# A convolution and attention trunk: tanh for sigmoid in the gate, norm sums on TensorE, first-half gate products on VectorE

## The chip, the cores and the metric

One core of one Trainium2 chip. The metric is the device time of one execution of the whole program in microseconds; the engines are called by the names of the profile: PE (TensorE), DVE (VectorE), ACT (ScalarE), POOL (GpSimd) and SP (SyncE, which issues most DMAs).

## What is computed

Two pre-norm residual layers over 1024 tokens with 16 meta tokens ahead (T = 1040 columns), model width 1024: a Conformer convolution layer, then a differential attention layer, then a last norm. The change lies in the convolution layer alone (CONV_WIDTH 2048, 31 taps):

```python
def conv_mixer(h, w_in, dw_kernel, dw_bias, ln_gain, ln_bias, w_out):
    proj = jnp.einsum("bld,dc->blc", h, w_in)
    u, g, z = jnp.split(proj, 3, axis=-1)
    v = u * jax.nn.sigmoid(g)
    v = lax.conv_general_dilated(v, dw_kernel[:, None, :], window_strides=(1,),
        padding=[(CONV_KERNEL - 1, 0)], dimension_numbers=("NWC", "WIO", "NWC"),
        feature_group_count=CONV_WIDTH) + dw_bias
    v = jax.nn.silu(layer_norm(v, ln_gain, ln_bias))
    return jnp.einsum("ble,ed->bld", v * jax.nn.silu(z), w_out)

# in the trunk, for layer i:
hn = rms_norm(h, norm_gain[i])
h = h + conv_mixer(hn, ...)
```

## The kernel before

Channels lie on partitions, tokens along the free axis. Every matmul operand is split into a high part (`hh`, `wh`, `b` hi: a rounded copy made by ACT) and a low part (`hl`, `wl`, `b` lo: the difference, made by `lo_part` on DVE or POOL), and `passes` issues three matmuls for each product. The tile scheduler sets the order of every engine's instructions from the written order and from priorities: `SP_R`, `HP` and `WP` are offsets that move what stands under them ahead. Each engine runs its list strictly in order.

*Start.* The 8 tiles of x (`x0` to `x7`) come in three chunks of tokens (348, 346, 346 columns). `unscaled` splits a chunk of raw x, `statistics` squares it and adds the squares over channels for the first RMS norm (`SUE` says for each chunk and tile whether an add runs on POOL, G, on DVE, V, or as a matmul with ones, P), `first_strips` (p) projects tile 0's g and u from the raw chunk, and `scaled` writes x times norm and gain and splits that again, for all later projections. `ORDER` gives the sequence of these steps. `rstd_from` turns the sums into a reciprocal root: a table estimate on ACT and a Newton step on DVE.

*Convolution loop.* For each of 16 tiles of 128 channels PE projects g and u; ACT takes the sigmoid `sig` of g; DVE multiplies it by u into `vr`, the gated input, kept as even and odd tokens. The 31 taps are split by parity: DVE runs the even ones and part of the combined ones (`ev`, `co`), ACT multiplies an odd tap into `pr` and POOL adds it to `pb`. PE also projects z; `z_gate` takes silu(z) on ACT and writes it to memory (`sz_d`), to be loaded later as `szr`. POOL adds the outputs up over tiles in `hsum` (the last tile's add is DVE's).

*Transition.* The tokens are treated in two halves. `channel_sums` makes means and variances on PE, `center` subtracts the mean on DVE and squares on ACT, `token_scale` makes the reciprocal root. `y_part(k, 0, ...)` multiplies by it (DVE), takes silu (ACT) and multiplies by `szr` (DVE for the numbers in `YM`, else POOL); `szr` tiles hold two channel tiles each and there are two of them. `operand` splits the result into b hi (ACT) and b lo (DVE). The first half's sixteen `y_part` are written first, then sixteen `operand`; then the output projection's eight strips `c0` to `c7` follow, each with two weights of eight channel tiles (`wh48`/`wl48` and so on). While the first half is multiplied, the second half is centred and made ready.

The table functions of ACT lie in sets that a table load of the engine exchanges; the program before has 36 such loads.

## Time and profile before

| | us |
|---|---|
| median of three runs | 1486.27 (1485.87 to 1486.83) |
| the profiled execution | 1487.72 |
| its span | 1485.9 |
| PE busy in the span | 1420.5 (96%) |
| DVE busy | 1139.7 (77%) |
| ACT busy | 898.3 (60%) |
| POOL busy | 861.4 (58%) |

The convolution layer takes the first 810 us or so, attention the next 530, the output projection the rest. The shares are averages over stages with different limits: in the convolution loop POOL and DVE are nearly full, in attention they are not. A line of a timeline gives start and length in us of a run of like instructions; the bracket at its end is the idle time of that engine ahead of it and what ended it.

### The profile page before, as it was taken

Reading aid. Unit: us, or ns where it says so; the run is one execution under the profiler, and the core shown is the slowest. Engines: PE = TensorE matmul, PEld = TensorE weight load, DVE = VectorE, ACT = ScalarE, POOL = GpSimd, SP = SyncE. Lnnn points to the kernel's source line nnn. Section 1 sums busy time; section 2 is a strip of 40 time slices with the busy share of each in tenths; the row PEclk is TensorE's granted clock in tenths of the full one; section 3 lists DMA queues with packets and bytes.
Section 4 is the critical chain, followed back from the end, with each engine's and each line's share of the span. In section 5 each row is a group of like instructions: output and inputs, shape, how many; then the busy total and the mean of one; then the engine's idle time right before and its main releaser. Section 6 shows DMA issues by size and latency. Waiting matters only on the chain.

```text
span 1485.9 us, 24104 instructions
## 1 busy us (share of the span) xinstructions
PE 1420.5 (96%) x8788; PEld 1330.1 (90%) x8788; DVE 1139.7 (77%) x2102; ACT 898.3 (60%) x1618; POOL 861.4 (58%) x677
## 2 busy tenths in 40 slices
PE   8899999999999999699999999999999999998997
PEld 6799899999999999699999877988889899897887
DVE  8999999989999989768645411477788787876774
ACT  5576666656565657746423511568778787787651
POOL 6499999999999942425113600525254354353572
PEclk9899999999999999799999999999999999999999
DMA  5011102111121232545444543322322322338642
GB/s 180 29 67 48 56 30 86 44 43 57 43 64 51 94 107 72 177 139 185 150 152 150 170 136 100 95 72 77 100 70 83 112 79 75 86 102 259 204 135 78
DMA packets 79928, 150.82 MB, mean 101 GB/s; under 512 B 6977, under 2 KB 46402, under 8 KB 78786
## 3 DMA queue, kind: packets, MB, share of 16 engines
q1 hardware_dynamic: 64802, 123.01, 26.0%
q0 software_dynamic: 5728, 17.04, 3.6%
q10 hardware_dynamic: 9280, 9.23, 1.9%
q8 instruction: 69, 1.13, 0.3%
q14 instruction: 49, 0.40, 0.1%
HBM read 106.73 MB, written 34.01 MB: 95 GB/s over the span
## 4 chain that ended last, share of the span: by engine, by line
PE 50%; POOL 19%; DVE 12%; issue 8%; ACT 7%; DMA 4%; ACTq 0%; POOLq 0%; DVEq 0%; SPq 0%
POOL pb L502 17%; PE c L209 8%; PE v L209 6%; PE z L209 6%; PE k L209 5%; PE q L209 4%; PE ao L209 4%; PE za L209 4%; PE o L209 3%; PE s L974 2%; PE tp L1008 2%; PE s L975 2%; DVE wl L159 1%; DMA a<-ya_d 1%; PE u L209 1%
## 5 line engine op out<-in xcount | busy, mean ns | idle before, releaser
L502 POOL TENSOR_TENSOR pb<-pr,pb 128x521 f32<-128x521 f32 (+1 forms) x272 | 388.2, 1437 | 15.7 <-ACT pr L501 1.1
L501 ACT ACTIVATE pr<-vr,chn 128x521 f32<-128x521 f32 x224 | 150.7, 724 | 115.6 <-POOL pb L502 115.0
L209 PE MATMUL c<-b,wh 128*128 128x260 f32 x1024 | 191.0, 289 | 11.0 <-DVE b L159 10.7
L191 ACT ACTIVATE wh<-wf 128x1024 fp32r<-128x1024 f32 x115 | 121.1, 1053 | 113.1 <-PE c L209 63.7
L515 DVE SCALAR_TENSOR_TENSOR ev<-vr,chn,ev 128x520 f32<-128x520 f32 x240 | 180.8, 754 | 1.3
L209 PEld LDWEIGHTS c<-b,wh 128*128 128x128 f32 x1024 | 162.9, 194 | 11.9 <-DVE b L159 11.2
L209 PE MATMUL g<-hp,wh 128*128 128x346 f32 (+1 forms) x752 | 149.2, 328 | 12.3 <-DVE sig L469 4.5
L159 DVE TENSOR_TENSOR wl<-wf,wh 128x1024 fp32r<-128x1024 f32 x81 | 130.7, 1613 | 36.4 <-ACT wh L191 35.2
L209 PE MATMUL u<-hp,wh 128*128 128x346 f32 (+1 forms) x752 | 149.7, 321 | 3.6 <-ACT sz L433 2.2
L209 PE MATMUL c<-b,wl 128*128 128x260 f32 x512 | 147.5, 290 | 5.5 <-DVE wl L159 5.5
L209 PEld LDWEIGHTS g<-hp,wh 128*128 128x128 f32 x752 | 125.8, 192 | 16.8 <-ACT n_r L234 4.7
L209 PE MATMUL z<-hp,wh 128*128 128x346 f32 (+1 forms) x768 | 135.7, 321 | 2.0 <-ACT sig L466 1.9
L159 POOL TENSOR_TENSOR wl<-wf,wh 128x1024 fp32r<-128x1024 f32 x34 | 84.1, 2473 | 92.0 <-ACT wh L191 43.7
L515 DVE SCALAR_TENSOR_TENSOR od<-xs,wc,od 128x520 f32<-128x520 f32 x176 | 132.3, 752 | 0.0
L209 PEld LDWEIGHTS u<-hp,wh 128*128 128x128 f32 x752 | 124.5, 188 | 4.9 <-ACT sz L433 2.4
L209 PEld LDWEIGHTS z<-hp,wh 128*128 128x128 f32 x768 | 124.2, 188 | 2.7 <-ACT sig L466 2.2
L982 ACT ACTIVATE p<-p,st 128x272 f32<-128x272 f32 (+7 forms) x128 | 100.5, 785 | 36.3 <-DVE st L977 35.6
L209 PEld LDWEIGHTS c<-b,wl 128*128 128x128 f32 x512 | 99.7, 195 | 6.3 <-DVE wl L159 6.2
L685 POOL TENSOR_TENSOR total<-hsq,total 128x520 f32<-128x520 f32 x12 | 20.7, 1724 | 117.8 <-ACT hsq L684 117.8
L209 PE MATMUL v<-wv,g 128*128 128x512 f32 x352 | 83.5, 394 | 0.0
L209 PE MATMUL g<-hp,wl 128*128 128x346 f32 (+1 forms) x376 | 81.9, 323 | 0.0
L974 PE MATMUL s<-k,q 128*128 128x256 f32 (+6 forms) x224 | 76.7, 347 | 3.7 <-DVE st L977 3.7
(295 smaller groups left out, 3525.7 us busy)
## 6 DMA issues: line engine op xcount, KB each, us to landing
wf<-conv_in SPq DMA_DIRECT2D x48, 512.0 KB, 3.5
wf<-conv_out SPq DMA_DIRECT2D x32, 512.0 KB, 3.8
wf<-attn_in SPq DMA_DIRECT2D x32, 512.0 KB, 3.6
wf<-attn_out SPq DMA_DIRECT2D x17, 512.0 KB, 3.6
sz_d<-sz ACTq DMA_DIRECT2D x32, 260.0 KB, 3.8
szr<-sz_d SPq DMA_DIRECT2D x16, 520.0 KB, 4.6
v<-v_d POOLq DMA_DIRECT2D x8, 1024.0 KB, 5.4
ya_d<-yb SPq DMA_DIRECT2D x28, 256.0 KB, 2.5
```

The costliest lines, as they stand in the source:

```text
L159: return eng.tensor_tensor(out=out_, in0=full, in1=hi, op=ALU.subtract)
L191: A.activation(out=wh, in_=wf, func=AF.Copy)
L209: PE.matmul(o, a[k], b[k], start=start and i == 0, stop=stop and i == tot - 1)
L501: A.activation(out=d, in_=src, func=AF.Copy, scale=w)
L502: G.tensor_tensor(out=dst, in0=d, in1=dst, op=ALU.add)
L515: V.scalar_tensor_tensor(out=dst, in0=src, scalar=w, in1=dst, op0=ALU.mult, op1=ALU.add)
L685: (V if SQA[m] == "V" else G).tensor_tensor(out=total[:, ns], in0=sq, in1=total[:, ns], op=ALU.add)
L974: PE.matmul(o[:, :wm], q2[m][:, qs], k2[m][:, c0 : c0 + wm], start=True, stop=False)
L975: PE.matmul(o[:, :wm], q2[m][:, qs], kl2[m][:, c0 : c0 + wm], start=False, stop=True)
L982: A.activation(out=p[:, :n], in_=p[:, :n], func=AF.Exp, scale=-1.0, bias=least, accum_out=st[:, 1:2],)
L1008: PE.transpose(tp[:, (kb - kb0) * P : (kb - kb0 + 1) * P], p0[:, kb * P : (kb + 1) * P], ident)
```

## The change

1. Sigmoid is computed as half of (1 + tanh of half the argument). The half is put into the taps once (`chn` times 0.5 for the 31 taps). Tanh lies in one table set with silu, which is loaded ahead of the first tanh; the changed program has 23 table loads. The gate product is (s + 1) times u in one DVE instruction; tile 0's product with the norm, which was POOL's, is now DVE's.
2. All 24 sums of squares of the first norm are matmuls with ones. The reciprocal root there, and the one of the convolution's norm, take Ln straight from the sums and two more operations on ACT, and two on DVE.
3. `ORDER` puts the first chunk's scaling ahead of the third chunk's strips; `SP_R` is 2000.
4. The last tile is not added to `hsum`; the mean's matmuls take `hsum` and the last tile as two terms.
5. All sixteen products with `szr` of the first half are on DVE. `y_part` and `operand` are written interleaved, with a lead of six tiles, and the second half's centring is gated from tile 2 on.

```diff
-YM = (5, 7, 11, 13, 15, 19, 23)
+YM = (*range(CT), 19, 23)
-SUE = "VPVPVPVP_GGGGGGGG_VGVGVGVG"
+SUE = "PPPPPPPP_PPPPPPPP_PPPPPPPP"
-SP_R = 200
-ORDER = "u0_t0_p0_u1_t1_p1_u2_t2_p2_s0_s1_s2"
+SP_R = 2000
+ORDER = "u0_t0_p0_u1_t1_p1_t2_s0_u2_p2_s1_s2"
+LEAD = 6
...
-        V.tensor_scalar(out=x, in0=sumps, scalar1=scale, scalar2=EPS, op0=ALU.mult, op1=ALU.add)
-        newton(x, r)
+        if not ahead:
+            V.tensor_scalar(out=x, in0=sumps, scalar1=scale, scalar2=EPS, op0=ALU.mult, op1=ALU.add)
+            newton(x, r)
+            return e
+        A.activation(out=x, in_=sumps, func=AF.Identity, scale=-0.5 * scale, bias=half_eps)
+        A.activation(out=t, in_=r, func=AF.Square)
+        V.tensor_tensor(out=x, in0=x, in1=t, op=ALU.mult)
+        V.scalar_tensor_tensor(out=r, in0=x, scalar=1.5, in1=r, op0=ALU.add, op1=ALU.mult)
...
+        V.tensor_scalar(out=chn[:, :, :TAPS], in0=chn[:, :, :TAPS], scalar1=0.5, scalar2=None, op0=ALU.mult)
...
-                    elif i:
-                        A.activation(out=s, in_=o, func=AF.Sigmoid)
+                    if i:
+                        A.activation(out=s, in_=o, func=AF.Tanh, scale=0.5)
...
-                            A.activation(out=s, in_=s, func=AF.Sigmoid)
-                        (V if SR == "V" else G).tensor_tensor(out=s, in0=s, in1=r, op=ALU.mult)
+                            if ci == 0:
+                                A.preload_act_table_set("silu_and_others")
+                            A.activation(out=s, in_=s, func=AF.Tanh, scale=0.5)
+                        V.scalar_tensor_tensor(out=s, in0=s, scalar=1.0, in1=r, op0=ALU.add, op1=ALU.mult)
...
-                        V.tensor_tensor(
-                            out=vr[:, par, PAD + s0 : PAD + s1], in0=u[:, o0:o1], in1=s[:, o0:o1], op=ALU.mult
-                        )
+                        dst = vr[:, par, PAD + s0 : PAD + s1]
+                        if i:
+                            V.scalar_tensor_tensor(
+                                out=dst, in0=s[:, o0:o1], scalar=1.0, in1=u[:, o0:o1], op0=ALU.add, op1=ALU.mult
+                            )
...
-            eng = V if i == CT - 1 else G
...
+            if 0 < i < CT - 1:
+                G.tensor_tensor(out=hsum, in0=v, in1=v_t[0] if i == 1 else hsum, op=ALU.add)
...
-                with tc.issue_after(gate[i >= 5]) if n else ExitStack():
+                with tc.issue_after(gate[i >= 2]) if n else ExitStack():
...
-            acc = channel_sums("mean_ps", hsum, n)
+            acc = channel_sums("mean_ps", (hsum, v_t[-1]), n)
...
-        full0 = [y_part(k, 0, False) for k in range(CT)]
-        operand(0, range(CT))
+        full0 = []
+        for k in range(CT + LEAD):
+            if k < CT:
+                full0.append(y_part(k, 0, False))
+            if k >= LEAD:
+                operand(0, [k - LEAD])
```

What stands in a row on an engine changes at many places of the start and the transition. On DVE ahead of the first chunk's scaling, before (`hp` is the split x, `sq` the squares, `rs_x` and `n0_r` the norm's argument and reciprocal root, `n0` its sums):

```order
L159 TENSOR_TENSOR hp6_101<-x6_93,hp6_101 128x346
L367 TENSOR_TENSOR sq2_116<-sq2_116,sq0_114 128x346
L367 TENSOR_TENSOR sq4_118<-sq4_118,sq2_116 128x346
L367 TENSOR_TENSOR sq6_120<-sq6_120,sq4_118 128x346
L237 TENSOR_TENSOR rs_x_203<-rs_x_203,n0_r_112 128x348
L238 SCALAR_TENSOR_TENSOR rs_x_203<-rs_x_203,n0_r_112 128x348
L239 SCALAR_TENSOR_TENSOR n0_r_112<-rs_x_203,n0_r_112 128x348
L217 TENSOR_SCALAR rs_x_293<-n0_122 128x346
L388 SCALAR_TENSOR_TENSOR x0_87<-x0_87,mod_76,n0_r_112 128x348
```

The same place after:

```order
L158 TENSOR_TENSOR hp5_100<-x5_92,hp5_100 128x346
L158 TENSOR_TENSOR hp6_101<-x6_93,hp6_101 128x346
L226 TENSOR_TENSOR rs_x_203<-rs_x_203,rs_t_204 128x348
L227 SCALAR_TENSOR_TENSOR n0_r_112<-rs_x_203,n0_r_112 128x348
L393 SCALAR_TENSOR_TENSOR x0_87<-x0_87,mod_76,n0_r_112 128x348
```

The three adds of squares and two of the four operations on the norm are gone between the last unscaled lo part and the first scaled x.

On ACT around tile 0's first gate, before (`wh2` and `wh3` are the hi parts of tile 1's two weights):

```order
L391 ACTIVATE hp2_97<-x2_89 128x348
L191 ACTIVATE wh2_167<-wf2_165 128x1024
L391 ACTIVATE hp3_98<-x3_90 128x348
...
L233 ACTIVATE rs_t_384<-rs_x_383 128x346
L191 ACTIVATE wh3_622<-wf3_620 128x1024
L234 ACTIVATE n0_r_112<-rs_t_384 128x346
L471 ACT_TABLE_LOAD
L471 ACTIVATE sig0_519<-sig0_519 128x348
```

And after:

```order
L219 ACTIVATE n0_r_112<-rs_t_368 128x346
L476 ACT_TABLE_LOAD
L225 ACTIVATE rs_t_368<-n0_r_112 128x346
L477 ACTIVATE sig0_520<-sig0_520 128x348
L190 ACTIVATE wh2_167<-wf2_165 128x1024
L477 ACTIVATE sig0_526<-sig0_526 128x346
L190 ACTIVATE wh3_624<-wf3_622 128x1024
```

Both weights moved behind the table load and the first gate.

On DVE in the transition around the first lo part of b (`mean` marks a centring of the second half), before:

```order
L610 TENSOR_TENSOR v5_2079<-v5_2079,szr4_0_5996 128x2x260
L551 TENSOR_TENSOR v12_4237<-v12_4237,mean_5544 128x2x260
L551 TENSOR_TENSOR v13_4495<-v13_4495,mean_5544 128x2x260
L551 TENSOR_TENSOR v14_4753<-v14_4753,mean_5544 128x2x260
L610 TENSOR_TENSOR v7_2683<-v7_2683,szr6_0_6004 128x2x260
L159 TENSOR_TENSOR b0_0_6044<-v0_614,b0_0_6044 128x2x260
L159 TENSOR_TENSOR b0_0_6044<-v1_871,b0_0_6044 128x2x260
```

And after:

```order
L559 TENSOR_TENSOR v15_5013<-v15_5013,mean_5545 128x2x260
L622 TENSOR_TENSOR v4_1823<-v4_1823,szr4_0_6001 128x2x260
L622 TENSOR_TENSOR v5_2081<-v5_2081,szr4_0_6001 128x2x260
L622 TENSOR_TENSOR v6_2427<-v6_2427,szr6_0_6009 128x2x260
L158 TENSOR_TENSOR b0_0_6014<-v0_616,b0_0_6014 128x2x260
L622 TENSOR_TENSOR v7_2685<-v7_2685,szr6_0_6009 128x2x260
L158 TENSOR_TENSOR b0_0_6014<-v1_873,b0_0_6014 128x2x260
```

Every product with `szr` now stands in DVE's list, the centring of tile 15 has come ahead of the first lo part, and between the start of y and that lo part lie 39 instructions. From the third strip of the first half on, the lists of all engines read alike in both programs.

## Rows read from the trace of the kernel before

**Rows 1.** The page: chain that ended last, shares by line.

```profile
POOL pb L502 17%; PE c L209 8%; PE v L209 6%; PE z L209 6%; PE k L209 5%; PE q L209 4%; PE ao L209 4%; PE za L209 4%; PE o L209 3%; PE s L974 2%; PE tp L1008 2%; PE s L975 2%; DVE wl L159 1%; DMA a<-ya_d 1%; PE u L209 1%
```

**Rows 2.** Stretches: length, busy PE, PEld, DVE, ACT, POOL, PE clock, DMA share, GB/s.

```profile
80.00:280.00 200.00, 195.93 (x1233) 194.81 (x1232) 194.20 (x272) 128.12 (x193) 193.34 (x132) 1.00 0.17 55
280.00:480.00 200.00, 193.39 (x1212) 191.96 (x1212) 188.67 (x275) 123.04 (x183) 193.49 (x131) 1.00 0.17 55
...
600.00:620.00 20.00, 9.18 (x43) 8.67 (x44) 18.69 (x19) 18.84 (x29) 9.95 (x6) 0.59 0.63 199
620.00:640.00 20.00, 20.00 (x155) 20.00 (x154) 16.62 (x25) 8.04 (x12) 1.31 (x1) 0.91 0.62 206
...
660.00:680.00 20.00, 20.00 (x169) 20.00 (x168) 17.64 (x21) 11.32 (x16) 8.25 (x6) 1.00 0.57 186
```

**Rows 3.** Groups of POOL, 75 to 540 us: busy us, mean ns, idle before.

```profile
L502 POOL TENSOR_TENSOR pb<-pr,pb 128x521 f32<-128x521 f32 (+1 forms) x272 | 388.2, 1437 | 15.7 <-ACT pr L501 1.1
```

**Rows 4.** Timeline of POOL in the start: start us, length us, instruction, idle before.

```profile
30.36 3.50 POOL L367 TENSOR_TENSOR sq<-sq,sq 128x346 f32<-128x346 f32 x3
...
74.56 6.76 POOL L502 TENSOR_TENSOR pb<-pr,pb 128x521 f32<-128x521 f32 x4 [1.09 <-ACT pr L501]
```

**Rows 5.** Timeline of DVE in the start.

```profile
24.84 5.93 DVE L159 TENSOR_TENSOR hp<-x,hp 128x346 fp32r<-128x346 f32 x5
...
31.90 3.62 DVE L159 TENSOR_TENSOR hp<-x,hp 128x346 fp32r<-128x346 f32 x5
...
37.52 0.52 DVE L237 TENSOR_TENSOR rs_x<-rs_x,n_r 128x348 f32<-128x348 f32 x1
...
39.49 5.39 DVE L388 SCALAR_TENSOR_TENSOR x<-x,mod,n_r 128x348 f32<-128x348 f32 x8
...
72.59 0.51 DVE L474 TENSOR_TENSOR vr<-gu,sig 128x346 f32<-128x346 f32 x1
```

**Rows 6.** Timeline of PE in the transition.

```profile
607.29 0.58 PE L209 MATMUL c<-b,wh 128*128 128x260 f32 x1 [9.99 <-DVE b L159]
...
617.74 0.58 PE L209 MATMUL c<-b,wl 128*128 128x260 f32 x1 [2.87 <-DVE wl L159]
```

**Rows 7.** Timeline of PE in the start (n: sums, g, u, z: projections).

```profile
13.70 0.85 PE L363 MATMUL n<-sq,ones 128*128 128x348 f32 x2 [1.25 <-DVE sq L360]
14.12 1.68 PE L209 MATMUL g<-hp,wh 128*128 128x348 f32 x8
...
51.08 4.98 PE L209 MATMUL g<-hp,wh 128*128 128x348 f32 x16 [4.46 <-DVE sig L469]
...
78.44 1.75 PE L209 MATMUL z<-hp,wh 128*128 128x348 f32 x10
```

**Rows 8.** Groups of ACT over the span: table loads of the sigmoid's line.

```profile
L466 ACT ACT_TABLE_LOAD x6 | 7.7, 1283 | 0.1
```

**Rows 9.** Timeline of DVE, end of the convolution and transition.

```profile
539.21 1.24 DVE L525 TENSOR_TENSOR hsum<-v,hsum 128x1040 f32<-128x1040 f32 x1
...
579.72 9.85 DVE L601 TENSOR_TENSOR v<-v,ln_r 128x520 f32<-128x520 f32 x16
...
601.92 4.09 DVE L551 TENSOR_TENSOR v<-v,mean 128x520 f32<-128x520 f32 x3
...
606.55 4.74 DVE L159 TENSOR_TENSOR b<-v,b 128x520 fp32r<-128x520 f32 x4
...
633.06 0.69 DVE L159 TENSOR_TENSOR b<-v,b 128x520 fp32r<-128x520 f32 x1
```

**Rows 10.** Timeline of POOL in the transition.

```profile
583.69 16.20 POOL L610 TENSOR_TENSOR v<-v,szr 128x520 f32<-128x520 f32 x4 [47.06 <-ACT v L602]
...
627.09 1.31 POOL L610 TENSOR_TENSOR v<-v,szr 128x520 f32<-128x520 f32 x1 [10.48 <-DMA szr<-sz_d]
```

**Rows 11.** The page: DMA issues of the gate's loads, KB, median us to landing.

```profile
szr<-sz_d SPq DMA_DIRECT2D x16, 520.0 KB, 4.6
```

More of the change, by code (lines that the diff above doesn't have):

```diff
@@ L210, in passes, with rstd_from @@
                 i += 1
-    def rstd_from(sumps, r, scale, c0, w, tmp=None, direct=False):
+    def rstd_from(sumps, r, scale, c0, w, tmp=None, direct=False, ahead=False):
         x, t = tmp or (small("rs_x", w=w), small("rs_t", w=w))
@@ L238, in newton @@
         V.scalar_tensor_tensor(out=x, in0=x, scalar=-0.5, in1=r, op0=ALU.mult, op1=ALU.mult)
-        return V.scalar_tensor_tensor(out=r, in0=x, scalar=1.5, in1=r, op0=ALU.add, op1=ALU.mult).ins
+        V.scalar_tensor_tensor(out=r, in0=x, scalar=1.5, in1=r, op0=ALU.add, op1=ALU.mult)
     def project(w, hh, hl, bank, chunks, release=False):
@@ L461, in trunk @@
                     s = small(f"sig{i}", w=w)
-                    if i == 0 and f"u{ci}" not in ORDER:
-                        with tc.issue_after(last_exp):
-                            A.activation(out=s, in_=o, func=AF.Sigmoid)
-                    elif i:
-                        A.activation(out=s, in_=o, func=AF.Sigmoid)
+                    if i:
+                        A.activation(out=s, in_=o, func=AF.Tanh, scale=0.5)
                     else:
@@ L533, in trunk, with channel_sums @@
         HK = CT // 2
-        def channel_sums(name, t, n):
+        def channel_sums(name, terms, n):
             acc = pair(f"{name}{n}").rearrange("p (two c) -> p two c", two=2)[:, :, :QT]
             with tc.high_priority(offset=WP):
-                for par in range(2):
-                    PE.matmul(acc[:, par], ones, part(t, n)[:, par], start=True, stop=True)
+                for j, t in enumerate(terms):
+                    for par in range(2):
+                        PE.matmul(acc[:, par], ones, part(t, n)[:, par], start=j == 0, stop=j == len(terms) - 1)
             return acc
@@ L564, in token_scale @@
                     A.preload_act_table_set("natural_log_exp_and_others")
[L565 removed]
                 with tc.issue_after(silus[0]), tc.issue_after(silus[-1]):
[L567 to L568 removed]
+                    A.activation(out=x, in_=acc, func=AF.Ln, scale=1.0 / CW, bias=eps)
+                    A.activation(out=r, in_=x, func=AF.Exp, scale=-0.5)
+                    e = A.activation(out=rr, in_=r, func=AF.Square).ins
+                    A.activation(out=x, in_=acc, func=AF.Identity, scale=-0.5 / CW, bias=half_eps)
+                V.tensor_tensor(out=x, in0=x, in1=rr, op=ALU.mult)
+                V.scalar_tensor_tensor(out=r, in0=x, scalar=1.5, in1=r, op0=ALU.add, op1=ALU.mult)
+            return e
         for n in range(2):
[L571 removed]
+            acc = channel_sums("mean_ps", (hsum, v_t[-1]), n)
             with tc.high_priority(offset=WP):
```

19 lines of the change are left out of this document (6 added, 13 removed).

## The prediction

> **What bounds the kernel now.** I read the page's chain first, then a table of stretches, then three places instruction by instruction. The chain of what ended last [rows 1] is mostly TensorE (PE) matmuls, but its largest single item is a GpSimd (POOL) line: the tap additions of the convolution, 17% of the span. The table [rows 2] says the same by stage. Between 80 and 480 us, the convolution loop, POOL is busy 386.8 of 400 us and PE 389.3; PE's missing 4.1 + 6.6 = 10.7 us are the slack it has there. POOL's content is one line, 272 products of 1.44 us [rows 3]. So this loop is paced by POOL, with PE and VectorE (DVE) close behind, and it ends earlier only if POOL starts earlier. POOL starts on it at 74.56 [rows 4], after DVE has written the last piece of tile 0's gated input (72.59) [rows 5].
>
> The one big hole is the window 600 to 620: PE is busy 9.18 of 20 us, its granted clock is 0.59, while DVE and ScalarE (ACT) are at 18.7 and 18.8 [rows 2]. The convolution's output is being normalised, gated and split into hi and lo there, and the output projection's matmuls wait for it: 9.99 us for the first lo part, 2.87 us for a weight's lo part [rows 6]. From 660 on PE runs dense, 169 matmuls in 20 us, and the order of the work behind this point is nearly the same in both kernels, so I take what is won by then as kept to the end.
>
> **The change, part by part. Start.** Three things leave DVE's path to the first scaling (39.49) [rows 5]. POOL's ten adds of squares go (the last three take 3.50 us) [rows 4]; beside them, DVE's lo parts took 5.93 us for five and 3.62 for the next five, 1.19 and 0.72 each [rows 5]. At 0.5 each, the price of their like once POOL rests (the newton steps between 37.52 and 39.49 are four operations in 1.97 us), ten save 4.5 us; the new halving of the taps is one operation of 496 elements a row, some 0.6 us by the same rate, so 3.9 remains. DVE's last adds, from 35.5 to 37.52, go: 2.0 us. Four operations become two: 1.0 us. Together 6.9 us at most. If the lo parts stay as slow, because ACT's hi parts set their pace, only 3.0 - 0.6 = 2.4 is left. I take 6.5, near the upper end, since the slow lo parts are just those that ran beside POOL's adds.
>
> The price is on PE: 24 fp32 sum matmuls instead of 8. One costs the distance from 13.70 to the next matmul at 14.12, 0.42 us [rows 7]: 16 more cost 6.7 us. They sit in the start, in which PE has idle time, and before g1, which now starts at 51.08 after a wait of 4.46 us [rows 7]. That start does not come earlier: ACT makes tile 1's weight wh2 behind the first tanh now, no longer ahead of it. By the order I get g1's start at 52 to 53 and the first z matmul near 80 in place of 78.44. PE then starts the loop 1 to 2 us late, and pays it out of its 10.7 us of slack. The Trainium skill ("FP8 and Floating Point Precision", TensorE Precision Notes) says that a true fp32 matmul makes four passes through the array, which speaks against moving sums to TensorE. The row shows 0.42 us for a sum; by four passes at the 0.159 us that a matmul takes in the loop (195.93 us for 1233) [rows 2] a sum would be about 0.64 (an estimate from that page) and the addition 10 us in place of 6.7, still in idle time.
>
> From the first scaling to POOL's start DVE's list keeps its length (three gate products arrive from POOL, four newton steps and one wait leave), so POOL starts about 6.5 us earlier, near 68.
>
> **Convolution loop.** Sigmoid becomes tanh, same instruction count; the gate product becomes one scalar-tensor-tensor of the same shape as the product it replaces. Both are priced at nothing: ACT and DVE do the same number of passes. Thirteen table loads fewer of 1.28 us each [rows 8] are 16.7 us of ACT. ACT is not the bound (it waits for POOL in the loop), so I count none of it. If ACT's cover is thinner than I think, this is a gain of some of the 10.7 us, on PE's side only. The 6.5 us are then carried: POOL ends 6.5 earlier, PE's slack falls from 10.7 by 6.5 and by the 1.5 late start, to about 3.
>
> **End of the convolution.** DVE's last add to hsum (1.24 us) [rows 9] goes, and PE takes eight more records for the two means instead: about equal, nothing. Token scale: two of five DVE operations go, some at least hidden beside ACT's; I take 0.5.
>
> **Transition.** Before, the products y times gate were split: eleven on POOL, five on DVE. POOL's first four took 4.05 us each while DVE multiplied beside it [rows 10], and DVE, multiplying at 0.616 us alone (9.85 for 16), took 1.36 for a centering (4.09 for three) and 1.19 for a lo part (4.74 for four) when POOL was at it [rows 9]. So both engines paid. After, all sixteen are on DVE: eleven more of 0.61 are 6.7 us, and the slow ones fall back to 0.61, at least 2.3 + 2.3 us in these two rows. In the new order the first lo part comes 39 DVE instructions after the start of y: 37 of 0.61 and two weight parts, twice as wide, of 1.2: 25.0 us; before it was 606.55 - 579.72 = 26.8 [rows 9]. Gain 1.8, with the 7.0 carried 8.8: first lo part at 597.7. The last is 33 rows further, four of them weights: 22.5 us more, 620.2, against 633.06 before [rows 9]; I add 3 for waits on the gate's loads: 623.
>
> PE: before, two restarts at a low clock and two waits. The 43 matmuls of 600 to 620 took 9.18 us, where 43 x 20/169 = 5.1 would do; the next window shows 155 in place of 169, 1.7 us more [rows 2]. That is 5.8 us for the clock. After, the weight of the second strip is ready soon after the first lo part, so one wait of 2.87 [rows 6] and half of the 5.8 should go: 5.8 together. Against this, PE reaches the last operands nearly as soon as they are made (623), and I take 2.1 off, a choice between nothing and those 3 us of waits. Sum: 8.8 + 5.8 - 2.1 = 12.5 us.
>
> The Trainium skill ("SBUF — State Buffer", Who interferes with whom) says that a DVE instruction with two inputs in SBUF contends with a GpSimd one that reads SBUF. The rows of the slow lo parts and products agree with it [rows 9, 10]; by it the second half, where GpSimd keeps most products, gains nothing.
>
> **Sum.** The profiled execution is 1487.72 us (span 1485.9); minus 12.5 is 1475.2. The median of the runs lies 1.45 below the profiled one, so the forecast is 1473.8 us. Its bounds: start 2.4 to 6.9, transition 2 (only the lo parts) to 10, that is 4.4 to 16.9 us: 1469.4 to 1481.9.
>
> **Rivals.** *Only one of the two gains arrives* (0.20). If POOL's earlier start is not carried, because DVE or PE is the next limit in the loop (DVE is busy 383 of the 400 us [rows 2]) or g1 comes later than I think, the transition alone is left: 12.5 - 6.5 = 6.0, 1480.3 us.
>
> *DVE blocks on the gate's loads: slower* (0.12). DVE runs in order. Before, a product that waited for its silu(z) back from memory stopped only POOL (10.48 us before the last one) [rows 10]; now it stops the lo parts behind it. Two buffers hold these loads, and each lands 4.6 us after its issue [rows 11]. Four loads (tiles 8 to 15) are issued only when DVE has used up an earlier pair. With none of this hidden DVE loses 4 x 4.6 = 18.4 us: last lo part at 620.2 + 18.4 = 638.6 in place of 633.06, 5.5 us later, 1491.8 us. It decides from 13 us of such waits on. Against it: the order puts 8 to 13 DVE instructions between the freeing of a buffer and its next use, 5 to 8 us.
>
> *No net change* (0.06). The strips behind are paced by something else than PE (weights' lo parts on DVE, the second half's products), and what is won at 630 is given back by 720: 1486.3 us.
>
> **How the numbers follow.** Forecast 0.62, its neighbour with one gain 0.20, slower 0.12, none 0.06. Both first cases are faster: 0.82. A measurement of this kernel tells apart about 0.2%, 3 us. The range must leave out at most 0.2: it leaves out the two last cases, covers the forecast's bounds and the 1480.3 with some 3 us of play: 1467 to 1484.
>
> **What would show it.** POOL's first tap product near 68 instead of 74.56, and its last as much earlier; first scaling on DVE near 33; PE's z matmuls ending near 590; the first lo part at about 598 and the last at about 623, with centerings and lo parts at 0.61 us each; one low-clock restart of PE, not two; window 640 to 660 at 169 matmuls. I am wrong if POOL starts early but PE's matmuls in the loop show new waits, if DVE's products in the transition wait for loads, or if the gain at 640 is not there at 820.

## The result, and the profile after

The changed kernel takes 1469.47 us (median; 1468.01 to 1470.63) against 1486.07 for the kernel before in the same session: a ratio of 0.9885, with a 95% interval of 0.9865 to 0.9906. The forecast was 1473.8 us, so the direction and the range hold, and the gain is larger than the 12.5 us that I summed. The profiled execution took 1470.63 us, its span is 1468.9 us: 17.0 us less than the 1485.9 before. All differences below are between these two profiled executions unless a ratio stands beside them.

The page of the changed kernel, engines' totals and the chain that ended last (to set beside [rows 1]):

```profile
PE 1425.6 (97%) x8828; PEld 1335.9 (91%) x8828; DVE 1113.2 (76%) x2100; ACT 887.0 (60%) x1615; POOL 817.6 (56%) x653
...
POOL pb L512 16%; PE c L208 8%; PE v L208 6%; PE q L208 5%; PE k L208 5%; PE za L208 5%; PE ao L208 4%; PE o L208 3%; ACT pr L511 2%; PE u L208 2%; PE z L208 2%; DVE wl L158 2%; PE s L990 2%; PE s L991 2%; PE tp L1024 2%
```

The tap additions on POOL lead the chain still, at 16%. ACT's products ahead of them (`pr`, 2%) are new in the list and PE's `u` rose from 1% to 2%, while PE's `z` fell from 6% to 2%: the chain passes through several engines in both kernels, and after the change more often through ACT. The stretches of the changed kernel (length, busy PE, PEld, DVE, ACT, POOL, PE clock, DMA share, GB/s), to set beside [rows 2]:

```profile
40.00:60.00 20.00, 18.25 (x105) 17.87 (x104) 20.00 (x31) 13.97 (x27) 9.87 (x8) 0.91 0.07 27
...
80.00:280.00 200.00, 197.54 (x1241) 196.35 (x1240) 182.86 (x268) 119.18 (x184) 190.14 (x130) 1.00 0.18 58
280.00:480.00 200.00, 197.70 (x1235) 197.13 (x1234) 187.62 (x275) 115.01 (x178) 191.90 (x131) 0.99 0.15 50
...
580.00:600.00 20.00, 16.95 (x95) 16.30 (x94) 20.00 (x31) 19.01 (x29) 0.00 (x0) 0.84 0.60 187
600.00:620.00 20.00, 20.00 (x168) 20.00 (x168) 19.65 (x31) 11.60 (x18) 0.00 (x0) 0.99 0.64 212
```

In the loop (80 to 480) PE went from 389.3 busy us to 395.2 of 400 and POOL from 386.8 to 382.0: PE's slack of 10.7 us is down to 4.8, and POOL, which missed 13.2 of the 400 us, now misses 18.0. In the transition 600 to 620 held 43 matmuls at a clock of 0.59, and now holds 168 at 0.99. The hole has become smaller and has moved ahead: 580 to 600 now holds 95 matmuls at 0.84, where it held 106 at 1.00.

Where the 17 us arise, read from the first instruction of each kind in the two timelines (before, after, and how much earlier):

| point | before | after | earlier, us |
|---|---|---|---|
| DVE: first scaling of x | 39.49 | 29.98 | 9.5 |
| POOL: first tap product | 74.56 | 65.37 | 9.2 |
| POOL: end of its last operation of the loop | 536.6 | 530.2 | 6.4 |
| DVE: the mean | 544.05 | 534.40 | 9.65 |
| DVE: first y | 579.72 | 568.94 | 10.8 |
| DVE: first lo part of b | 606.55 | 593.81 | 12.7 |
| third strip of the output projection written | 651.70 | 632.04 | 19.7 |
| last strip written | 807.09 | 787.13 | 20.0 |
| span | 1485.9 | 1468.9 | 17.0 |

### The profile page after: what moved, and what is told of

It is laid out like the page before. It is cut to its first block, busy times and chain, and to the rows that moved or that the text cites. A ratio compares the mean times of both kernels' runs of the same rounds, so it can differ in the third digit from the quotient of the medians.

```text
span 1468.9 us, 24139 instructions
## 1 busy us (share of the span) xinstructions
PE 1425.6 (97%) x8828; PEld 1335.9 (91%) x8828; DVE 1113.2 (76%) x2100; ACT 887.0 (60%) x1615; POOL 817.6 (56%) x653
## 4 chain that ended last, share of the span: by engine, by line
PE 50%; POOL 17%; DVE 13%; ACT 8%; issue 8%; DMA 4%; SPq 0%; POOLq 0%; DVEq 0%; ACTq 0%
POOL pb L512 16%; PE c L208 8%; PE v L208 6%; PE q L208 5%; PE k L208 5%; PE za L208 5%; PE ao L208 4%; PE o L208 3%; ACT pr L511 2%; PE u L208 2%; PE z L208 2%; DVE wl L158 2%; PE s L990 2%; PE s L991 2%; PE tp L1024 2%
## 5 line engine op out<-in xcount | busy, mean ns | idle before, releaser
L208 PE MATMUL u<-hp,wh 128*128 128x346 f32 (+1 forms) x752 | 155.9, 321 | 2.1 <-ACT wh L190 2.1
L158 DVE TENSOR_TENSOR wl<-wf,wh 128x1024 fp32r<-128x1024 f32 x81 | 118.9, 1469 | 29.7 <-ACT wh L190 29.0
L697 POOL TENSOR_TENSOR total<-hsq,total 128x520 f32<-128x520 f32 x12 | 20.6, 1715 | 196.1 <-DMA xr<-xn 99.2
```

What stands on the lines that cost most here:

```text
L158: return eng.tensor_tensor(out=out_, in0=full, in1=hi, op=ALU.subtract)
L208: PE.matmul(o, a[k], b[k], start=start and i == 0, stop=stop and i == tot - 1)
L697: (V if SQA[m] == "V" else G).tensor_tensor(out=total[:, ns], in0=sq, in1=total[:, ns], op=ALU.add)
```

## The experiments

Twelve kernels ran. Five leave out one part of the change, two make one part alone, two give POOL extra work, and three move single pieces of the order. Each ratio is to the kernel before on the same chip in the same session; the changed kernel's own is 0.9885.

| kernel | ratio (95%) | span, us | POOL's first product | first lo part | third strip |
|---|---|---|---|---|---|
| only_start | 0.9966 (0.9953 to 0.9979) | 1481.8 | 72.1 | 603.7 | 645.7 |
| only_trans | 0.9953 (0.9936 to 0.9969) | 1480.1 | 74.3 | 602.7 | 640.5 |
| no_start | 0.9932 (0.9914 to 0.9949) | 1477.0 | 76.5 | 601.0 | 641.9 |
| no_trans | 0.9951 (0.9931 to 0.9972) | 1480.8 | 66.0 | 598.9 | 642.4 |
| no_tanh | 0.9886 (0.9868 to 0.9905) | 1472.3 | 71.9 | 599.0 | 637.3 |
| no_norm | 0.9905 (0.9883 to 0.9928) | 1468.7 | 65.4 | 594.1 | 632.1 |
| delay_before | 1.0050 (1.0031 to 1.0068) | 1492.5 | 78.0 | 615.4 | 657.2 |
| delay_after | 0.9891 (0.9868 to 0.9914) | 1473.5 | 68.8 | 599.0 | 636.8 |
| no_tanh_last | 0.9880 (0.9852 to 0.9908) | 1472.0 | 66.6 | 597.1 | 635.5 |
| no_ym | 0.9928 (0.9905 to 0.9950) | 1477.1 | 66.1 | 602.3 | 642.0 |
| gate8 | 0.9898 (0.9872 to 0.9924) | 1469.9 | 65.4 | 588.3 | 632.3 |
| gate8late | 0.9893 (0.9872 to 0.9915) | 1469.6 | 65.9 | 588.7 | 633.0 |

### Each half alone, and each half left out

only_start: the kernel before, with the new sums, root and order of the start (the branch `ahead` of `rstd_from`, shown under The change, comes with it).

```diff
-SUE = "VPVPVPVP_GGGGGGGG_VGVGVGVG"
+SUE = "PPPPPPPP_PPPPPPPP_PPPPPPPP"
-SP_R = 200
-ORDER = "u0_t0_p0_u1_t1_p1_u2_t2_p2_s0_s1_s2"
+SP_R = 2000
+ORDER = "u0_t0_p0_u1_t1_p1_t2_s0_u2_p2_s1_s2"
...
-                return rstd_from(acc, n0_r, 1.0 / D, c0, w, None, DIR0[ci])
+                return rstd_from(acc, n0_r, 1.0 / D, c0, w, None, True, True)
```

> The kernel before with the start's part alone (all sums of squares on TensorE, two-operation reciprocal root, the new order of the first steps). Theory (the start's gain is carried through the loop by POOL, and TensorE has 10.7 us of slack there): POOL's first tap product near 66, the loop's last one 6 us earlier than in the kernel before, time 1479 to 1481. Rival (TensorE is the loop's limit, the start's gain is lost): under 2 us faster, 1484 to 1486.

only_trans: the kernel before, with the products on DVE, the interleaved writing and the earlier gating.

```diff
-YM = (5, 7, 11, 13, 15, 19, 23)
+YM = (*range(CT), 19, 23)
+LEAD = 6
...
-                with tc.issue_after(gate[i >= 5]) if n else ExitStack():
+                with tc.issue_after(gate[i >= 2]) if n else ExitStack():
...
-        full0 = [y_part(k, 0, False) for k in range(CT)]
-        operand(0, range(CT))
+        full0 = []
+        for k in range(CT + LEAD):
+            if k < CT:
+                full0.append(y_part(k, 0, False))
+            if k >= LEAD:
+                operand(0, [k - LEAD])
```

> The kernel before with the transition's part alone (all sixteen first-half gate products on VectorE, the interleaved writing, the earlier gate). Theory (both engines paid for sharing, and TensorE restarts once instead of twice): 8 to 10 us faster, 1476 to 1478, with nothing earlier before 580 us. Rival (the products cost VectorE as much as they save): within 2 us of before.

no_start and no_trans are the changed kernel with one of these two diffs taken back.

```diff
-SUE = "PPPPPPPP_PPPPPPPP_PPPPPPPP"
+SUE = "VPVPVPVP_GGGGGGGG_VGVGVGVG"
-SP_R = 2000
-ORDER = "u0_t0_p0_u1_t1_p1_t2_s0_u2_p2_s1_s2"
+SP_R = 200
+ORDER = "u0_t0_p0_u1_t1_p1_u2_t2_p2_s0_s1_s2"
...
-                return rstd_from(acc, n0_r, 1.0 / D, c0, w, None, True, True)
+                return rstd_from(acc, n0_r, 1.0 / D, c0, w, None, DIR0[ci])
```

> The changed kernel without the start's part. Theory: it loses what the start alone gains, 6 us: 1475 to 1477. Rival (the loop is paced by something else, so that the start is worth nothing): 1469 to 1471.

```diff
-YM = (*range(CT), 19, 23)
+YM = (5, 7, 11, 13, 15, 19, 23)
-LEAD = 6
...
-                with tc.issue_after(gate[i >= 2]) if n else ExitStack():
+                with tc.issue_after(gate[i >= 5]) if n else ExitStack():
...
-        full0 = []
-        for k in range(CT + LEAD):
-            if k < CT:
-                full0.append(y_part(k, 0, False))
-            if k >= LEAD:
-                operand(0, [k - LEAD])
+        full0 = [y_part(k, 0, False) for k in range(CT)]
+        operand(0, range(CT))
```

> The changed kernel without the transition's part. Theory: it loses 8 to 10 us: 1477 to 1480. Rival (what comes earlier out of the loop is enough, and the transition ends with the last loads from memory): under 3 us lost, 1469 to 1472.

Alone the start gives 0.34% and the transition 0.47%, 5.1 and 7.0 us; left out of the changed kernel they cost 0.47 and 0.66 points of the ratio, 7.0 and 9.8 us. Both gains are real: each interval lies clear of 1, and the rival with only one of the two falls. At the third strip, ahead of the stretch whose length scatters by 4 us (below), the transition alone is 11.3 us earlier than before and everything but the transition (start, tanh and norm together) 9.3, in sum 20.6 where the whole change shows 19.7. The start and the transition alone do not make up the whole: 12.1 of 17.1 us by the ratios (the intervals leave the size of this gap open), 6.0 + 11.3 = 17.3 of 19.7 at the third strip. only_trans stays below the 8 to 10 us expected, though its interval reaches 9.5.

only_start missed what was expected of it. It moves the first scaling by the full 9.3 us (39.5 to 30.2), but POOL's first product only by 2.4, and POOL's last operation of the loop ends at 535.7, 0.9 us earlier than before, not 6. Of the 6.0 us at the third strip only 0.9 can thus have come through POOL; the first lo part is 2.8 us earlier, the last one 5.3 (627.8 against 633.1), in a transition whose code is that of the kernel before. That the start's gain is carried by POOL is not what this run shows. POOL's timeline in only_start:

```profile
72.13 7.66 POOL L508 TENSOR_TENSOR pb<-pr,pb 128x521 f32<-128x521 f32 x5 [2.02 <-ACT pr L507]
```

Something between the scaling and POOL, which the start alone doesn't move, holds POOL back. The next pair finds it.

### The tanh, and the place of one matmul

no_tanh is the changed kernel with sigmoid, POOL's product with the norm, and the plain gate product (not shown: the table load ahead of the first tanh goes, and the product into `vr` of the other tiles becomes plain too).

```diff
-        V.tensor_scalar(out=chn[:, :, :TAPS], in0=chn[:, :, :TAPS], scalar1=0.5, scalar2=None, op0=ALU.mult)
...
-                        A.activation(out=s, in_=o, func=AF.Tanh, scale=0.5)
+                        A.activation(out=s, in_=o, func=AF.Sigmoid)
...
-                        V.scalar_tensor_tensor(out=s, in0=s, scalar=1.0, in1=r, op0=ALU.add, op1=ALU.mult)
+                        (V if SR == "V" else G).tensor_tensor(out=s, in0=s, in1=r, op=ALU.mult)
```

> The changed kernel with the sigmoid back (and its table loads, the gate's plain product, tile 0's product on POOL). Theory (ACT is not the loop's limit, table loads are idle time of ACT): under 2 us lost, 1469 to 1472. Rival (table loads in front of the gate hold TensorE's banks, whose waits for the sigmoid were 3.1 + 1.9 us in the kernel before): 4 to 8 us lost, 1473 to 1478.

Its ratio, 0.9886, is the changed kernel's. By the two profiled executions it is 3.4 us longer and by the third strip 5.3, and the interval of the ratio is some 3 us to either side: the tanh is worth between nothing and about 4 us. What it clearly does is to start POOL: without it that is 6.5 us later, at 71.9, just where only_start has it. DVE's timeline there:

```profile
61.35 6.36 DVE L522 SCALAR_TENSOR_TENSOR ev<-vr,chn,ev 128x520 f32<-128x520 f32 x8
67.62 0.51 DVE L476 TENSOR_TENSOR sig<-gu,n_r 128x346 f32<-128x346 f32 x1
...
69.95 0.52 DVE L481 TENSOR_TENSOR vr<-gu,sig 128x346 f32<-128x346 f32 x1
```

and what PE does ahead of it:

```profile
62.75 0.32 PE L210 MATMUL gu<-hp,wl 128*128 128x346 f32 x1
```

POOL's first product needs the whole row of `vr`. The last piece comes from `gu`, tile 0's third chunk, and the last of the 24 matmuls of `gu`'s u strip stands alone in no_tanh's PE list, 80 rows behind its predecessor and behind tile 1's first strips. It runs at 62.75. By then DVE has begun eight tap products that don't need it (61.35, 6.36 us), and only behind them it scales `gu` (67.62). In only_start the same three rows stand at 62.92, 61.54 and 67.81. In the changed kernel DVE's timeline has the scaling ten us sooner:

```profile
57.47 0.50 DVE L473 TENSOR_TENSOR sig<-gu,n_r 128x346 f32<-128x346 f32 x1
...
63.41 0.50 DVE L486 TENSOR_TENSOR vr<-gu,sig 128x346 f32<-128x346 f32 x1
```

no_tanh_last moves this one matmul forward by the scheduler's priority and changes nothing else in the code of no_tanh; the scheduler then also puts DVE's scaling of `gu` ahead of the tap products (59.32).

```diff
-                PE.matmul(o, a[k], b[k], start=start and i == 0, stop=stop and i == tot - 1)
+                last = flag and i == tot - 1
+                with tc.high_priority(offset=1000) if last else ExitStack():
+                    PE.matmul(o, a[k], b[k], start=start and i == 0, stop=stop and i == tot - 1)
...
+                flag[:] = [1] if ci == 2 and n == 1 else []
```

> The sigmoid kept as in no_tanh (the changed kernel with the sigmoid back), but tile 0's very last matmul of the third chunk stands directly behind its predecessor in TensorE's list instead of 80 rows later, behind tile 1's first two strips of g and u. Theory (the sigmoid kernel lost POOL's early start by the place of this one matmul, not by table loads): POOL's first tap product near 66 instead of 71.9, the loop's end 4 to 6 us earlier than in no_tanh, time 2 to 5 us less than there. Rival (sigmoid and its table loads hold the gate): first product stays near 72, no gain.

POOL's timeline there:

```profile
66.56 11.96 POOL L515 TENSOR_TENSOR pb<-pr,pb 128x521 f32<-128x521 f32 x8 [4.22 <-ACT pr L514]
```

So the place of the matmul, with the order on DVE that follows it, held POOL back: 71.94 becomes 66.56, 5.4 of the 6.5 us, with the sigmoid still in place. Editing the gate's arithmetic had moved the scheduler's list; the 1.2 us that remain are not accounted for. But the loop ends only 1.9 us earlier (533.5 against 535.4), and the ratio doesn't move (0.9880). The second half of the theory, that an earlier POOL start is time won at the end of the loop, holds here only to a third.

### Is a shift of POOL carried through the loop?

Five copies of the first tap tile onto itself stand ahead of POOL's first product, 4.1 us in the kernel before and 3.7 in the changed one. The results don't change.

```diff
+                    if i == 0 and n == 0:
+                        for _ in range(5):
+                            G.tensor_copy(out=dst, in_=dst)
```

> The kernel before with five copies of a tile onto itself on POOL ahead of its first tap product, 5 to 7 us of POOL time; the result is unchanged. Theory (POOL paces this loop in the kernel before): nearly all of it lost, 4 to 7 us, 1490 to 1493. Rival (TensorE paces it, POOL catches up): under 2 us lost.

> The changed kernel with the same five copies on POOL. Theory (after the change TensorE and ACT take part in the pace, since POOL started 9.2 us earlier and ended only 6.4 us earlier): about half of it lost, 2 to 4 us, 1472 to 1474. Rival (POOL still paces alone): 5 to 7 us lost, 1475 to 1477.

POOL's timeline in delay_before, and then in delay_after:

```profile
73.77 4.14 POOL L497 COPY pb<-pb 128x521 f32<-128x521 f32 x5 [0.47 <-ACT pb L494]
77.99 7.21 POOL L505 TENSOR_TENSOR pb<-pr,pb 128x521 f32<-128x521 f32 x4
```

```profile
64.97 3.70 POOL L507 COPY pb<-pb 128x521 f32<-128x521 f32 x5 [4.50 <-ACT pb L504]
68.75 6.58 POOL L515 TENSOR_TENSOR pb<-pr,pb 128x521 f32<-128x521 f32 x4
```

The first product comes 3.4 us later in both. The kernel before pays in full and more: the loop ends 5.5 us later (542.1) and the time rises by 7.4 us, ratio 1.0050; where the 2.1 us beyond the delay at the loop's end and the further 1.9 in the time come from I did not trace. The changed kernel pays 2.4 us at the loop's end (532.7), 0.7 per us, and 0.0006 of the ratio, which can't be told from nothing. So in the kernel before a later POOL is paid for, while the changed one takes up a part. What an earlier or later start does at the loop's end differs much between these pairs: 0.9 of 2.4 us in only_start, 1.9 of 5.4 between no_tanh and no_tanh_last, 2.4 of 3.4 here, 5.5 of 3.4 in delay_before. Each is one execution of lists that the edit has also reordered, so a single factor is not shown. POOL's group in the changed kernel, 75 to 540 us (busy, mean ns, idle before), beside [rows 3]:

```profile
L512 POOL TENSOR_TENSOR pb<-pr,pb 128x521 f32<-128x521 f32 (+1 forms) x266 | 381.2, 1443 | 19.4 <-ACT pr L511 5.2
```

A product costs the same (1443 against 1437 ns), but idle time rose from 15.7 to 19.4 us, and the part of it that ends with ACT's `pr` from 1.1 to 5.2. The 1.1 all stand ahead of the very first product [rows 4], and the row above begins six products into the loop: within the loop POOL did not wait for `pr` before, and waits 5.2 us for it now. The loop became 2.8 us longer (9.2 won at its start, 6.4 at its end). Which engine holds ACT's `pr` back, PE or ACT itself, I did not separate.

### The mean

no_norm takes the two-term mean and the shorter root behind the convolution back (the root's lines are left out here).

```diff
-            if 0 < i < CT - 1:
-                G.tensor_tensor(out=hsum, in0=v, in1=v_t[0] if i == 1 else hsum, op=ALU.add)
+            eng = V if i == CT - 1 else G
+            if i == 1:
+                eng.tensor_tensor(out=hsum, in0=v_t[0], in1=v, op=ALU.add)
+            elif i > 1:
+                eng.tensor_tensor(out=hsum, in0=v, in1=hsum, op=ALU.add)
...
-            acc = channel_sums("mean_ps", (hsum, v_t[-1]), n)
+            acc = channel_sums("mean_ps", hsum, n)
```

> The changed kernel without the two-term mean and the shorter reciprocal root of the convolution's norm. Theory (the last add to hsum and three VectorE operations lay on the path between the convolution and the first y: y started 4.4 us earlier than the loop's end explains): 3 to 5 us lost, 1472 to 1475. Rival (as I predicted, an equal exchange): under 1 us lost.

The mean comes 1.3 us later than in the changed kernel, the first y 1.5, the third strip 0.05, and the ratio of 0.9905 lies inside the changed kernel's interval. So the exchange is worth 1.3 us where it stands and nothing that shows behind it; the profiled execution of no_norm is the fastest of its four, and the medians would allow some 3 us. Yet between the loop's end and the mean the changed kernel won 3.2 us. PE's rows for the mean, in the kernel before and in the changed one:

```profile
542.54 1.92 PE L540 MATMUL mean_ps<-hsum,ones 128*128 128x260 f32 x8
```

```profile
531.03 1.15 PE L548 MATMUL mean_ps<-hsum,ones 128*128 128x260 f32 x4 [1.14 <-DVE v L528]
```

Before, `hsum` was complete at 540.45 [rows 9], and the matmuls stood 2.1 us further on in PE's list; after, PE waits 1.14 us for the data and goes at once. Two of the three us are thus the place in the list. The chain that ended last says the same. In the kernel before, from 480 to 545 us, it runs through PE's `z` up to the mean and not through POOL at all:

```profile
487.33 55.36 PE z L209 x349
```

After the change it reaches the mean through POOL's last operation (528.94) and `v` (530.27). POOL's end was thus not what the mean waited for before, although POOL leads the chain over the whole loop. delay_after shows how chancy that place is: the same code, with POOL's list five copies longer, has its mean split in two:

```profile
536.82 1.04 PE L551 MATMUL mean_ps<-hsum,ones 128*128 128x260 f32 x4
...
539.24 1.04 PE L551 MATMUL mean_ps<-hsum,ones 128*128 128x260 f32 x4
```

and the mean on DVE comes 8.5 us behind the loop's end, where the changed kernel has 4.2 and the kernel before 7.4.

### Sharing the gate products with POOL

no_ym changes one line of the changed kernel: the products with `szr` go back to POOL, all but five.

```diff
-YM = (*range(CT), 19, 23)
+YM = (5, 7, 11, 13, 15, 19, 23)
```

> The changed kernel with the first half's gate products shared again, eleven on POOL and five on VectorE; all else as changed. Theory (sharing makes both engines slow: POOL 4 us for a product, VectorE twice its time for centring and lo parts): first lo part 3 to 6 us later, two restarts of TensorE, 4 to 7 us lost against the changed kernel. Rival (the interleaving and the earlier start do it, where a product runs doesn't matter): under 2 us lost.

Its ratio gives 10.7 us won in place of 17.1, so that the sharing costs 6.4 us; the first lo part is 8.5 us later. POOL's timeline in no_ym, its DVE groups from 570 to 640, and the same groups of the changed kernel:

```profile
573.63 17.40 POOL L622 TENSOR_TENSOR v<-v,szr 128x520 f32<-128x520 f32 x4 [42.78 <-ACT v L614]
```

```profile
L158 DVE TENSOR_TENSOR b<-v,b 128x520 fp32r<-128x520 f32 x16 | 12.5, 826 | 1.9 <-ACT b L639 1.9
L559 DVE TENSOR_TENSOR v<-v,mean 128x520 f32<-128x520 f32 x14 | 12.1, 926 | 0.0
...
L622 DVE TENSOR_TENSOR v<-v,szr 128x520 f32<-128x520 f32 x5 | 3.4, 687 | 6.4 <-DMA szr<-sz_d 6.4
```

```profile
L158 DVE TENSOR_TENSOR b<-v,b 128x520 fp32r<-128x520 f32 x16 | 10.5, 689 | 0.0
L622 DVE TENSOR_TENSOR v<-v,szr 128x520 f32<-128x520 f32 x16 | 10.3, 690 | 0.0
...
L559 DVE TENSOR_TENSOR v<-v,mean 128x520 f32<-128x520 f32 x14 | 8.7, 692 | 0.0
```

Beside POOL the centring costs 926 ns in place of 692 and the lo part 826 in place of 689, while POOL's own product, 1.31 us by itself [rows 10], is stretched to 4.35 us. The Trainium skill ("SBUF — State Buffer", Who interferes with whom) says that a DVE instruction with two inputs in SBUF contends with a GpSimd one that reads SBUF; these rows agree. With all products on DVE no load is waited for at all; with five there DVE waits 6.4 us for one, a larger part of the 8.5 than the slower instructions. Eleven more products on one engine made that engine's list shorter in time, not longer. PE pays for the mixed order with two restarts, by its timeline in no_ym:

```profile
598.27 0.59 PE L208 MATMUL c<-b,wh 128*128 128x260 f32 x1 [6.92 <-ACT sz L438]
603.00 0.58 PE L208 MATMUL c<-b,wh 128*128 128x260 f32 x1 [4.14 <-DVE b L158]
```

The matmul behind each wait takes 0.58 or 0.59 us; behind two short waits later in the same run (0.33 us at 608.27, 0.23 at 609.50), with the clock up again, it takes 0.39. The window 600 to 620 has a granted clock of 0.84 there, part of it at the lower of the two levels (1.2 and 2.4 GHz), and 117 matmuls, against 0.99 and 168.

### Does the first lo part set the end of the transition?

In the changed kernel PE's last waits end with the first lo part of `b` (594.56, below). My theory was that bringing this part forward brings the third strip forward by as much; the rival, that DVE's whole list up to the last lo part sets it. gate8 holds the second half's centring of tiles 8 to 15 back until the fourth operand is done, gate8late until the eighth.

```diff
-                with tc.issue_after(gate[i >= 2]) if n else ExitStack():
+                with tc.issue_after(gate[(i >= 2) + (i >= 8)]) if n else ExitStack():
...
-        center(1, [added[0], y_mult[CT - 1]])
+        center(1, [added[0], y_mult[CT - 1], done[3]])
```

> The changed kernel with the second half's centring of tiles 8 to 15 gated behind the first half's fourth lo part, so that eight centrings leave the path to the first lo part (about 5 us). Theory (the first lo part at 593.8 comes 3.5 us after the last z matmul and causes TensorE's pause and its slow clock until 600): first lo part near 588, no pause, no slow clock, 4 to 6 us less than the changed kernel, 1464 to 1466. Rival (VectorE's whole list up to the last lo part sets the strips' end, so only the waiting moves): within 1.5 us of the changed kernel.

```diff
-        center(1, [added[0], y_mult[CT - 1]])
+        center(1, [added[0], y_mult[CT - 1], done[7]])
```

> As gate8, but the eight centrings stand behind the eighth lo part, where gate8 left TensorE a wait of 2.60 us for the fifth and a slow clock after it. Theory (TensorE, not VectorE, ends the transition, and loses there what it pauses and what the slow clock takes): no wait for a lo part, third strip's end 3 to 4 us earlier than in the changed kernel and in gate8 (628 to 629 against 632), time 2 to 4 us less than the changed kernel if nothing behind takes it back. Rival (VectorE's whole list sets the end, a wait moves to the later lo parts): third strip's end at 631 to 633, within 1.5 us of the changed kernel.

DVE's timeline in gate8, and PE's in gate8 and in gate8late:

```profile
588.33 1.31 DVE L158 TENSOR_TENSOR b<-v,b 128x520 fp32r<-128x520 f32 x2
```

```profile
598.24 0.39 PE L208 MATMUL c<-b,wh 128*128 128x260 f32 x1 [2.60 <-DVE b L158]
```

```profile
605.75 1.03 PE L208 MATMUL c<-b,wh 128*128 128x260 f32 x5 [0.91 <-ACT wh L190]
...
610.06 0.39 PE L208 MATMUL c<-b,wh 128*128 128x260 f32 x1 [0.86 <-DVE b L158]
```

The first lo part comes 5.5 and 5.1 us earlier, just as wanted. In gate8 the wait of 2.60 us moves the low clock behind it (0.87 from 600 to 610); in gate8late PE is spared it (1.00 from 580 to 620). The last lo part still starts at 615.5 and 616.5, against 616.1 in the changed kernel, the third strip comes at 632 to 633, and the times are no better (0.9898 and 0.9893). The wait has only moved to a later operand. My theory fell. That DVE's list as a whole sets the end fits, but is not shown to be all: in gate8late PE's two longest waits (0.96 and 0.91 us) end with ACT's `wh`, and its third strip is done on PE at 631.5, 0.9 us earlier than in the changed kernel, and written only after DVE has waited 1.33 us for the load of `xr`.

## Why the prediction was right, and where it missed

**Start: mechanism right, the term too small.** I took 6.5 us for the first scaling and for POOL, with 6.9 as the most; it was 9.5 and 9.2. The timeline of DVE in the start, three adds of squares of the kernel before that I had passed over:

```profile
13.57 1.24 DVE L367 TENSOR_TENSOR sq<-sq,sq 128x348 f32<-128x348 f32 x1
...
16.94 0.51 DVE L367 TENSOR_TENSOR sq<-sq,sq 128x348 f32<-128x348 f32 x1
...
17.80 0.51 DVE L367 TENSOR_TENSOR sq<-sq,sq 128x348 f32<-128x348 f32 x1
```

and of the changed kernel, beside [rows 5]:

```profile
15.46 7.34 DVE L158 TENSOR_TENSOR hp<-x,hp 128x348 fp32r<-128x348 f32 x10
22.73 0.41 DVE L445 TENSOR_SCALAR chn<-chn 128x496 f32<-128x496 f32 x1
...
26.00 2.24 DVE L158 TENSOR_TENSOR hp<-x,hp 128x346 fp32r<-128x346 f32 x5 [1.97 <-ACT hp L384]
28.82 0.58 DVE L226 TENSOR_TENSOR rs_x<-rs_x,rs_t 128x348 f32<-128x348 f32 x1 [0.58 <-ACT rs_t L225]
29.43 0.52 DVE L227 SCALAR_TENSOR_TENSOR n_r<-rs_x,n_r 128x348 f32<-128x348 f32 x1
29.98 6.08 DVE L393 SCALAR_TENSOR_TENSOR x<-x,mod,n_r 128x348 f32<-128x348 f32 x8
```

Twenty lo parts stand ahead of the scaling from 8.5 us on, in both kernels. They took 21.6 us before and take 15.3 now (0.73 each in the row of ten, 0.45 in the last five): 6.2 saved, where I had 4.5 from the ten that I had shown. All the adds of squares go, not only the last three: 2.0 and 2.1, so 4.1 in place of 2.0. The norm gives 1.2 (1.0 expected), the copy of the taps 0.7, the halving costs 0.3 (0.6 expected). New waits for ACT take 2.5 back. That is 9.4 of the 9.5 us measured. The term began too late: I read the path from 24.84 on, and it begins at 8. That POOL's start moved as far as the scaling does not follow from the path that I gave: in only_start the scaling came 9.3 us earlier and POOL 2.4, held by the one matmul above, whose place in the changed kernel I had not checked.

**z on PE: the sign was wrong.** I had PE starting the loop 1 to 2 us late (first z near 80); it started 4.2 us early. PE's timeline in the start, beside [rows 7]:

```profile
26.21 4.82 PE L368 MATMUL n<-sq,ones 128*128 128x346 f32 x16
30.60 1.37 PE L208 MATMUL g<-hp,wl 128*128 128x346 f32 x6
...
49.73 4.67 PE L208 MATMUL g<-hp,wh 128*128 128x348 f32 x18 [1.75 <-ACT wh L190]
...
74.22 2.87 PE L208 MATMUL z<-hp,wh 128*128 128x348 f32 x17
```

The chain that I named holds: g1 waits for ACT's weight, now behind the first tanh. But I left the times of ACT as they were, although the same earlier statistics let the table load and the tanh come sooner. ACT's timeline:

```profile
46.56 1.28 ACT L476 ACT_TABLE_LOAD   x1
...
48.26 0.48 ACT L477 ACTIVATE sig<-sig 128x348 f32<-128x348 f32 x1
48.64 1.04 ACT L190 ACTIVATE wh<-wf 128x1024 fp32r<-128x1024 f32 x1
```

g1 therefore starts at 49.73, not 52 to 53, after 1.75 us of waiting in place of 4.46, and the clock of 40 to 60 is 0.91 in place of 0.74. A fp32 sum costs more than the 0.42 us of my row: eight of them (16 records) fill 26.21 to 30.60, 0.55 us each, so sixteen more cost 8.8 us at that price, in place of 6.7; PE still started the loop earlier. The Trainium skill ("FP8 and Floating Point Precision", TensorE Precision Notes) speaks of four passes for true fp32; the estimate of 0.64 us made from it lay above what these rows show, my single row below.

**Loop: "carried in full" failed in part.** Of 9.2 us, 6.4 reached the end. That this is near the 6.5 in the sum is luck, since two errors cancel: the start was worth 2.7 more, and only 0.7 of each us was carried. delay_before agrees with full carrying in the kernel before, from whose trace I argued; only_start (0.9 of 2.4 us) does not, and in delay_after 2.4 of 3.4 us came through. PE's slack fell to 4.8 us, not to 3.

**End of the convolution: 0 and 0.5 expected; 3.2 and 1.1 measured.** The exchange itself came out near nothing, as predicted; most of the gain is the place of the mean's matmuls in PE's list, which I had not looked at: I took POOL's end for the end of the loop, and in the kernel before PE's list ended it.

**Transition on DVE: right.** From the first y to the first lo part 2.0 us were won, 1.8 expected; the first lo part itself is at 593.8 in place of 597.7 because of the terms before it. In a row the centrings take 0.62 us each (4.97 for eight from 582.29 on), as forecast, and the last lo part starts at 616.1, not 623: the 3 us that I added for loads, and the price that the slower rival was made of, are not there. No wait for `szr` shows on DVE in the changed kernel.

**PE in the transition: direction right, term too small.** From the first lo part to the third strip 6.9 us were won, where 5.8 - 2.1 = 3.7 were expected. PE's timeline, beside [rows 6]:

```profile
591.22 0.38 PE L208 MATMUL c<-b,wh 128*128 128x260 f32 x1 [0.49 <-ACT sz L438]
592.51 0.39 PE L208 MATMUL c<-b,wh 128*128 128x260 f32 x1 [0.90 <-ACT wh L190]
594.56 0.58 PE L208 MATMUL c<-b,wh 128*128 128x260 f32 x1 [1.66 <-DVE b L158]
```

Three waits of 3.05 us together and one stretch of slow matmuls (594.56 to about 600) stand where waits of 9.99 and 2.87 us and two such stretches of about that length stood. The deduction of 2.1 us, for operands that PE would catch up with, was not needed: the last lo part came 7 us sooner than I had put it.

**Behind the transition: 3.0 us given back, which I had at nothing.** The last strip of the output projection comes 20.0 us earlier, the span ends 17.0 earlier. From the third strip on PE's matmuls stand in the same order in both, so the lead can be followed from one to the next: it is 20.2 us up to 989.5 us of the changed kernel, 18.7 at 992.9, 18.9 at 1418.9, and 16.9 from 1421.2 on. Two places of the changed kernel take most of it, a stretch at a lower clock, in the form of [rows 2], and a wait:

```profile
990.00:1000.00 10.00, 9.06 (x54) 8.00 (x54) 8.17 (x30) 6.93 (x14) 2.38 (x5) 0.86 0.52 174
```

```profile
1421.01 1.89 PE L208 MATMUL ao<-a,wh 128*128 128x256 f32 x14 [1.79 <-DVE f L1142]
```

The same matmuls run at a clock of 1.00 in the kernel before (1010 to 1020), behind the same wait of 1.76 us. At the second place the kernel before does not wait. DVE's `f` stands in DVE's list behind the lo part of the weight `wo_qk`; for that weight's load ACT waited 0.34 us before, and 2.60 us here. Neither place follows the change. The wait of 1.76 us stands in all fourteen traces, and a lower clock directly behind it in five of them (the changed kernel, only_trans, delay_before, delay_after, gate8late); the wait at the place of 1421 is at most 0.22 us in the other thirteen. From the seventh strip's write to the end the fourteen take 784.8 to 789.1 us, 786.4 before and 788.9 after, and no part of the change goes with it: no_trans and only_trans share no part and both lie high. The profiled execution of the changed kernel is also the slowest of its four. So the 3 us are of this execution, as far as these traces tell; what sets the clock or the load off in one execution and not in another is not shown.

**The rivals.** One gain alone: no, both arrive. DVE blocked by loads: no, no such wait. Nothing net: no. The sum was low by 4.5 us of span: between the loop's end and the mean 3.2, PE in the transition 3.2, token scale 0.6, DVE in the transition 0.2 and the last strips 0.3 were missing, and 3.0 given back stood on the other side; the start's term and the loop's carrying cancelled.

## What to carry to other kernels

Before pricing an edit, read where its neighbours stand in each engine's list: one matmul placed 80 rows later, and the order on DVE that went with it, held POOL's start back by 5.4 us, and the mean's place was worth 2 us, neither of them meant by the edit that moved it. When two engines share one phase's elementwise work, price the sharing from rows where both run at once; giving all of it to the one engine can shorten that engine's own list. And a shift is carried only as far as the pacing engine still paces: count the slack of the others after the gain, and follow the chain up to the very instruction that ends the stage.

## What the runs showed of the hardware

- DVE and POOL products slowed each other by very different shares: POOL's went from 1.31 us to 4.35, DVE's from 0.69 to 0.83 and 0.93.
- A fp32 matmul with 346 columns took 0.55 us in a dense row of eight, against 0.159 us for one matmul of the loop, a factor of 3.5; two in a row with 348 columns took 0.45 each (14.18 to 15.09 in the changed kernel).
- A table load of 1.28 us was followed by the next ACT instruction without a further pause: the load starts at 46.56, where the instruction ahead of it ends, and the next one starts at 47.86.
- The length of a wait didn't tell alone what PE's clock does behind it. Behind 1.66 us in the changed kernel, where PE had run three matmuls in the 4 us ahead, the first matmul already took 0.58 us; behind 2.60 us in gate8 the first took 0.39, and slow ones (0.42 where 0.28 is usual) began about 1 us later. The same wait of 1.76 us in the attention layer was followed by the lower clock in five traces of fourteen.
